# Queries and keys of a differential attention produced channel-major, rotated through a small DMA round trip

## The chip, the cores and the metric

The kernel runs on one core of a Trainium2 chip. The metric is device time in microseconds of one execution; three runs of the kernel before gave 909.8 to 910.3 us, median 910.19 us. A separate execution was profiled.

## The reference

Two layers over a sequence of 512 tokens and a width of 1024. A layer normalises the rows, multiplies them by a 1024 x 5120 matrix, and splits the result into ten blocks of 512 columns. Four mixers work on these: a state-space scan (S5), a differential attention with partial rotary positions, a gated linear recurrence (RG-LRU), and an attention into 256 memory tokens. Their gated results, 2048 wide, go through an output matrix and are added to the residual. The part that the change touches:

```python
for layer in range(DEPTH):                                   # DEPTH = 2
    h = rms_norm(x, norm_g[layer])
    proj = h @ w_in[layer]
    a_u, a_g, qd, kd, vd, b_g, c_x, c_g, m_q, m_g = jnp.split(proj, 10, axis=-1)
    ...
    q = rope_partial(qd.reshape(B, L, 4, 2, 64), cos, sin)   # turns dims 0..15 of each 64
    k = rope_partial(kd.reshape(B, L, 4, 2, 64), cos, sin)
    o_b = diff_attention(q, k, v, lam)       # softmax(q1 k1) - lam * softmax(q2 k2), causal
    y_b = rms_norm(o_b, da_subln_g[layer]) * (1 - lam_init)
```

## The kernel before

All large products are made with values split in two float32r parts: `w_split` casts a weight piece (128 x 1024) to `whi` on ACT (L168) and takes the remainder `wlo` on DVE (L174), and each product is three matmuls of 512 columns (high x high, high x low, low x high). A piece holds 24 matmuls, for memory values 12. There are 68 pieces a layer; raw pieces come by SP's queue into two buffers, `whi` and `wlo` have three buffers each, and DVE's and ACT's work for a piece is written two pieces ahead of its use.

A block of 512 projected columns is 96 matmuls. `tm_block` (L535) gives it token-major: a tile has 128 tokens in its partitions, four accumulators in PSUM are filled at once and evacuated at the block's end. `cm_block` (L515) gives it channel-major: a tile has 128 channels in its partitions and all 512 tokens along them; it goes in two units of two accumulators. `ORDER` lists the blocks of each layer by hand: `q v k kv cx au ...` in the first, `q k cx v kv au mq bg mg ...` in the second.

Between the matmuls, other work is written out by `Streams`: after every 12 matmuls of a block a `tick` goes by and each live generator makes one step; a generator that yields a number sleeps for so many ticks. A block of 512 columns is 8 ticks. Attention is such a stream, with an item (128 queries of one head, both softmaxes) every second tick, 16 items a layer and two further steps; S5, RG-LRU, the memory attention and the parameters are others. The compiler's scheduler then sets the order of each engine's instructions by this program order and by what it takes to be ready.

Before, q and k were made token-major. `qk_evac` copies an accumulator to `qz` (ACT, L575), multiplies dims 0 to 15 by cosines and sines (DVE, four small operations a token tile), and two ticks later `flush_qk` turns the tile to channel-major by four 128 x 128 transposes on TensorE (L595). From the transposed PSUM tile q is copied once (L598); k is copied and subtracted into two tiles `kT` whose halves hold its high and low parts (L603, DVE). `attention` starts when q, k and v are all there, which is after k in the first layer and after v in the second.

Tiles of 512 columns a partition that live long (`b8`) share 14 buffers, tiles of 4 KB (`b4`) four, tiles of 2 KB (`b2`) ten; in PSUM there are four accumulators (`acc`), two banks for transposes and small products (`tp` and `ms`), and one double bank for scores (`sc`).

At the start, SP's queue brings the first tile of x, constants, the second tile of x, the first weight piece, the third tile, the second piece and the fourth tile. `norm_h` and `transpose_split` normalise and transpose each tile.

Of the kernel before, what the change touches and what calls it, by code (L numbers as in the profile page):

```python
# [9 lines left out]
F32 = mybir.dt.float32  # L10
# [6 lines left out]
P = 128  # L17
D = 1024
# [8 lines left out]
ROPE_THETA = 500000.0  # L27


ORDER = ["q v k kv cx au cg bg mq ag mg gl oAM0 oAM1 oBC0 oBC1".split(),  # L30
         "q k cx v kv au mq bg mg ag cg gl oAM0 oAM1 oBC0 oBC1".split()]

C_ID, C_DM, C_IF, C_KEEP, C_CM, C_END = 0, 128, 144, 152, 152, 280

# [13 lines left out]


MEM_AHEAD = 2  # L50
BD_AHEAD = 3
S5P_AT = 2
D_MEM = (3, 2, 1)
D_S5 = (1, 1, 2, 2, 1, 2)
D_AT = 2


class Streams:
# [31 lines left out]
def tile_kernel(ctx: ExitStack, tc: tile.TileContext, A, out):  # L90
# [20 lines left out]
    def b8(shape, name, dtype=F32):  # L111
        return big.tile(shape, dtype, tag="b8", name=nm(name))
# [4 lines left out]
    def b2(shape, name, dtype=F32):  # L117
        return sm2.tile(shape, dtype, tag="b2", name=nm(name))
# [10 lines left out]
    def tp(shape=(P, 4, 128)):  # L129
        return ps.tile(list(shape), F32, tag="tp", bufs=2, name=nm("tp"))  # L130
# [13 lines left out]
    def w_dma(upto):  # L144

        while loaded[0] < min(upto, len(pieces)):
            w_load(loaded[0])
            loaded[0] += 1
# [12 lines left out]
    def w_split(i, pool_):  # L161

        while split[pool_] < min(i + 1, len(pieces)):
            j = split[pool_]
            split[pool_] += 1
            if pool_ == "hi":
                hi = wpool.tile([P, 1024], F32R, tag="whi", bufs=NHI, name=nm("whi"))
                S.copy(hi, wbuf[j])  # L168
                wbuf[j] = (wbuf[j], hi)
            else:  # L170
                w_split(j, "hi")
                raw, hi = wbuf[j]
                lo = wpool.tile([P, 1024], F32R, tag="wlo", bufs=NLO, name=nm("wlo"))
                V.tensor_tensor(out=lo, in0=raw, in1=hi, op=ALU.subtract)  # L174
                wbuf[j] = (hi, lo)
                w_dma(j + NRAW + 1)
# [5 lines left out]


    xr = A["x"].rearrange("o (t p) d -> p (o t) d", p=P)
    xd = ctx.enter_context(tc.tile_pool(name="xd", bufs=1, space=bass.MemoryType.DRAM)).tile([L, D], F32, tag="xd", name="xd")
    xdr = xd.rearrange("(t p) d -> p t d", p=P)
    xt = {}

# [32 lines left out]
    for l in range(DEPTH):  # L221
        for n in ORDER[l]:
            if n == "kv":
                for u in range(2):
                    add(l, "mk", u, cm_pieces(A["w_mem_kv"][l], 256 * u))
                add(l, "mv", 0, tm_pieces(A["w_mem_kv"][l], 512))
            elif n == "gl":
                w = A["s5_w_glu"][l].rearrange("(k p) (s c) -> p k s c", p=P, s=2)
                for u in range(2):
                    add(l, "gl", u, [w[:, 2 * i:2 * i + 2, :, 256 * u:256 * u + 256] for i in range(2)])  # L230
            elif n[0] == "o":
                ps_ = []
                for g in n[1:3]:
                    r0 = 512 * "ABCM".index(g)
                    ps_ += tm_pieces(w_out[l, r0:r0 + 512], 512 * int(n[3]))
                add(l, "o", n[1:], ps_)
            elif n in ("q", "k", "v", "au"):
                add(l, n, 0, tm_pieces(w_in[l], COL[n]))
            else:
                for u in range(2):  # L240
                    add(l, n, u, cm_pieces(w_in[l], COL[n] + 256 * u))
# [8 lines left out]
    S.dma_start(out=grow, in_=A["norm_g"][0:1, :])  # L250
    ident = cst[:, C_ID:C_ID + 128]
    nc.sync.dma_start(out=cst[:, C_ID:C_KEEP], in_=A["consts"][:, C_ID:C_KEEP])
    for t in range(1, NT):
        nc.sync.dma_start(out=xs(t), in_=xr[:, t, :])
        w_dma(t)
# [39 lines left out]
    def norm_h(t):  # L295

        h = b4([P, D], "h")
        r = rstd_of(xs(t), D, h)
        scale_h(h, t, r)
        return h  # L300
# [24 lines left out]

    new_hT()
    hn = norm_h(0)
    for t in range(NT):
        h, hn = hn, (norm_h(t + 1) if t + 1 < NT else None)
        transpose_split(h, cur["hi"], cur["lo"], t * 128)  # L330
        if t < 2:
            w_split(t, "lo")
# [16 lines left out]
    def tt(o, a, b, op):  # L349
        V.tensor_tensor(out=o, in0=a, in1=b, op=op)  # L350
# [63 lines left out]
    def params():  # L414
# [71 lines left out]
        V.tensor_scalar(out=cneg, in0=cpos, scalar1=-4.0, scalar2=None, op0=ALU.mult)  # L486
        V.tensor_scalar(out=cpos, in0=cpos, scalar1=4.0, scalar2=None, op0=ALU.mult)

    nsum = const.tile([P, NT], F32, tag="nsum", name="nsum")

    mrs = const.tile([P, 2], F32, tag="mrs", name="mrs")
# [30 lines left out]
    def tm_block(lhs, evac, ids, tiles=NT, late=False):  # L522


        hi, lo = lhs
        a = [acc() for _ in range(tiles)]
        np_ = len(ids)
        wv = {}

        def mm(p, t):  # L530
            whi, wlo = wv[p]
            for kk in range(2):
                k = 2 * p + kk
                for i, (h, w) in enumerate(((hi, whi), (hi, wlo), (lo, whi))):
                    PE.matmul(a[t], h(k, t), w[:, kk, :], start=(p == 0 and kk == 0 and i == 0),  # L535
                              stop=(p == np_ - 1 and kk == 1 and i == 2))
            if p == np_ - 1:
                evac(t, a[t])

        def take(p):  # L540
            wv[p] = [w.rearrange("p (k c) -> p k c", k=2) for w in w_use(ids[p])]

        for p in range(np_ - 2 if late else np_):
            take(p)
            for t in range(tiles):
                mm(p, t)
                if t % 2 == 1:
                    yield
        if late:
            take(np_ - 2)  # L550
            take(np_ - 1)
            for t in range(tiles):
                mm(np_ - 2, t)
                mm(np_ - 1, t)
                yield

    def h_cm():
        hi, lo = cur["hi"], cur["lo"]
        return (lambda k: hi[k // 4][:, k % 4, :]), (lambda k: lo[k // 4][:, k % 4, :])

    def h_tm():
        hi, lo = cur["hi"], cur["lo"]
        return ((lambda k, t: hi[k // 4][:, k % 4, t * 128:(t + 1) * 128]),
                (lambda k, t: lo[k // 4][:, k % 4, t * 128:(t + 1) * 128]))
# [4 lines left out]
        return ((lambda k, t: hi[k // 4][:, k % 4, t, :]), (lambda k, t: lo[k // 4][:, k % 4, t, :]))  # L569


    def qk_evac(dst):
        def f(t, a):
            z = b2([P, 8, 64], "qz")
            S.copy(z, a.rearrange("p (m d) -> p m d", d=64))  # L575
            z12 = z[:, :, 0:16].rearrange("p m (s f) -> p m s f", f=8)
            ca = rcos[:, t, :].unsqueeze(1).unsqueeze(1).to_broadcast([P, 8, 2, 8])
            sa = rsin[:, t, :].unsqueeze(1).unsqueeze(1).to_broadcast([P, 8, 2, 8])
            rab = b2([P, 2, 8, 2, 8], "rab")
            ra, rb = rab[:, 0], rab[:, 1]  # L580
            tt(ra, z12, ca, ALU.mult)
            tt(rb, z12, sa, ALU.mult)
            tt(z12[:, :, 0, :], ra[:, :, 0, :], rb[:, :, 1, :], ALU.subtract)
            tt(z12[:, :, 1, :], ra[:, :, 1, :], rb[:, :, 0, :], ALU.add)
            pend.append((dst, t, z, st.now))
        return f

    pend = []
    def flush_qk():

        while pend and st.now - pend[0][3] >= 2:
            dst, t, z, _ = pend.pop(0)
            pt = tp()
            for j in range(4):
                PE.transpose(pt[:, j, :], z[:, 2 * j:2 * j + 2, :].rearrange("p m d -> p (m d)"), ident)  # L595
            ts = slice(t * 128, (t + 1) * 128)
            if len(dst) == 1:
                S.copy(dst[0][:, :, ts], pt)  # L598
            else:

                for m in range(2):
                    own, oth = slice(m * 64, m * 64 + 64), slice(64 - m * 64, 128 - m * 64)
                    S.copy(dst[m][own, :, ts], pt[own])  # L603
                    tt(dst[m][oth, :, ts], pt[own], dst[m][own, :, ts], ALU.subtract)

    st.hook = flush_qk

    def attention(l, R):
        while pend or "par" in st.live:
            yield  # L610
        qT, kT, v = R["qT"][0], R["kT"], R["v"]
        o = qT
        R["o"] = o
        oss = const.tile([P, 16], F32, tag="oss", name=nm("oss"))
# [495 lines left out]
    def run(gen):  # L1110
        for _ in gen:
            st.tick()
# [30 lines left out]
    def s5p_start(l):  # L1143
        s5_load(l, Rl[l])
        st.start("s5p", s5_params(l, Rl[l]))

    st.start("par", params())
    s5p_start(0)
    for pi, (l, n, u, ids) in enumerate(plan):
        R = Rl[l]  # L1150
# [5 lines left out]
        if any(p[0] == l and p[1] == "cx" for p in plan[pi:pi + BD_AHEAD]) and "bd" not in R:  # L1156
            lru_load(l, R)
        if n in ("q", "k"):
            R[n + "T"] = [b8([P, 4, L], "qT")] if n == "q" else [b8([P, 4, L], "kT", F32R) for _ in range(2)]
            run(tm_block(h_tm(), qk_evac(R[n + "T"]), ids))  # L1160
        elif n == "v":
            vt = R["v"] = b8([P, NT, 512], "v")

# [78 lines left out]
        elif n == "gl":  # L1242
# [4 lines left out]
            for hf, pid in enumerate(ids):  # L1247
                whi, wlo = (w.rearrange("p (k s c) -> p k s c", k=2, s=2) for w in w_use(pid))
                for j in range(2):
# [13 lines left out]
                        ag = R["ag"][:, 2 * u + j, :]  # L1263
                        V.scalar_tensor_tensor(out=ag, in0=th, scalar=0.25, in1=ag, op0=ALU.mult, op1=ALU.mult)
                    st.tick()
        if n in ("q", "k", "v") and all(a in R for a in ("qT", "kT", "v")):
            st.start("attn", attention(l, R))
        if n == "o":
            pair, half = u[:2], int(u[2])
# [99 lines left out]
```

## Time and profile before

| | |
|---|---|
| median of three runs | 910.19 us |
| profiled execution | 911.01 us, of which the span from first to last instruction is 909.2 us |
| TensorE (PE) | busy 887.7 us, 98% |
| VectorE (DVE) | busy 667.3 us, 73% |
| ScalarE (ACT) | busy 510.7 us, 56% |
| GpSimd (POOL) | busy 42.2 us, 5% |
| DMA | 90.05 MB, 99 GB/s on average |
| granted clock of TensorE | 0.997 |

A busy PE is not a PE at its peak: matmuls are pipelined and each is shown with a duration longer than the distance to the next, so the distances between starts tell what one costs. Sums below are made against the profiled execution; the median of the runs is 0.8 us lower.

### The profile page before, as it was taken

What the parts mean: (1) busy time and instruction counts of PE and PEld (TensorE: products, weight loads), DVE (VectorE), ACT (ScalarE), POOL (GpSimd) and SP (SyncE); (2) the same over time, 40 slices, a digit from 0 to 9 for tenths busy, and PEclk for the clock granted to TensorE, in tenths of its full rate; (3) what the DMA queues carried; (4) which work ended last, traced back from release to release, by engine and by line L of the source; (5) the groups of instructions that cost most, each with busy time, mean ns of one, the idle gap of its engine ahead of it and who ended that gap; (6) DMA issues with size and microseconds to landing.
All of it is one profiled execution on the core that took longest, in us unless ns stands there. A gap on an engine that the chain in (4) does not pass through costs nothing.

```text
span 909.2 us, 12391 instructions
## 1 busy us (share of the span) xinstructions
PE 887.7 (98%) x4478; PEld 746.5 (82%) x4478; DVE 667.3 (73%) x1345; ACT 510.7 (56%) x1032; POOL 42.2 (5%) x86
## 2 busy tenths in 40 slices
PE   7999999999999999999999999999999999999996
PEld 5788878987878888888888888898888888788885
DVE  5984988778999956883384676875999996666343
ACT  5673786985344265921454468766656354863133
POOL 1001000001101100000100000000101110000000
PEclk9999999999999999999999999999999999999998
DMA  5743432022212236433343321432112222152322
GB/s 179 180 139 105 140 95 88 29 68 58 89 55 66 74 115 194 132 107 108 107 157 101 92 88 58 136 116 70 50 48 74 74 74 93 47 186 96 109 73 93
DMA packets 80929, 90.05 MB, mean 99 GB/s; under 512 B 23778, under 2 KB 58211, under 8 KB 80868
## 3 DMA queue, kind: packets, MB, share of 16 engines
q1 hardware_dynamic: 77842, 85.72, 30.1%
q10 hardware_dynamic: 722, 2.36, 0.8%
q0 software_dynamic: 2304, 1.18, 0.5%
q8 instruction: 35, 0.57, 0.3%
q14 instruction: 26, 0.21, 0.1%
HBM read 84.40 MB, written 4.19 MB: 97 GB/s over the span
## 4 chain that ended last, share of the span: by engine, by line
PE 73%; DVE 20%; ACT 5%; issue 2%; DMA 1%; SPq 0%; DVEq 0%; ACTq 0%
PE acc L535 38%; PE acc L515 16%; PE acc L1255 5%; DVE wlo L174 3%; DVE u L350 2%; DVE xr L1040 2%; DVE wt L350 2%; DVE xr L350 1%; PE ms L679 1%; PE tp L315 1%; PE sc L807 1%; PE sc L645 1%; PE tp L832 1%; PE sc L646 1%; DVE li L757 1%
## 5 line engine op out<-in xcount | busy, mean ns | idle before, releaser
L174 DVE TENSOR_TENSOR wlo<-raw,whi 128x1024 fp32r<-128x1024 f32 x136 | 166.0, 1221 | 120.8 <-ACT whi L168 117.0
L168 ACT CAST whi<-raw 128x1024 fp32r<-128x1024 f32 x136 | 143.2, 1053 | 190.4 <-PE acc L535 119.2
L515 PE MATMUL acc<-hThi,whi 128*128 128x512 f32 x384 | 153.3, 399 | 0.0
L515 PE MATMUL acc<-hThi,wlo 128*128 128x512 f32 x384 | 150.8, 393 | 0.0
L515 PE MATMUL acc<-hTlo,whi 128*128 128x512 f32 x384 | 150.6, 392 | 0.0
L535 PE MATMUL acc<-whi,hThi 128*128 128x512 f32 x256 | 104.1, 407 | 2.3 <-ACT whi L168 2.3
L535 PE MATMUL acc<-wlo,hThi 128*128 128x512 f32 x256 | 101.9, 398 | 0.0
L535 PE MATMUL acc<-whi,hTlo 128*128 128x512 f32 x256 | 101.1, 396 | 0.0
L535 PE MATMUL acc<-wlo,mxh 128*128 128x512 f32 x256 | 100.1, 391 | 0.0
L535 PE MATMUL acc<-whi,mxl 128*128 128x512 f32 x256 | 100.1, 391 | 0.0
L535 PE MATMUL acc<-whi,mxh 128*128 128x512 f32 x256 | 100.0, 391 | 0.0
L515 PEld LDWEIGHTS acc<-hThi,wlo 128*128 128x128 f32 x384 | 72.2, 188 | 14.8
L515 PEld LDWEIGHTS acc<-hTlo,whi 128*128 128x128 f32 x384 | 72.3, 188 | 13.3
L515 PEld LDWEIGHTS acc<-hThi,whi 128*128 128x128 f32 x384 | 72.2, 188 | 13.3
L535 PEld LDWEIGHTS acc<-whi,hThi 128*128 128x128 f32 x256 | 56.3, 220 | 10.3 <-ACT whi L168 2.7
L535 PEld LDWEIGHTS acc<-whi,hTlo 128*128 128x128 f32 x256 | 56.5, 221 | 7.8 <-DVE hTlo L318 0.2
L535 PEld LDWEIGHTS acc<-wlo,hThi 128*128 128x128 f32 x256 | 56.5, 221 | 7.2
L535 PEld LDWEIGHTS acc<-wlo,mxh 128*128 128x128 f32 x256 | 48.1, 188 | 9.8
L535 PEld LDWEIGHTS acc<-whi,mxl 128*128 128x128 f32 x256 | 48.1, 188 | 9.8
L535 PEld LDWEIGHTS acc<-whi,mxh 128*128 128x128 f32 x256 | 48.1, 188 | 9.6
L976 POOL DMA_DIRECT2D MT<-kq x64 | 32.1, 509 | 486.2 <-DVE kq L350 336.6
L655 ACT ACTIVATE e<-sc,nmx 128x128 f32<-128x128 f32 (+3 forms) x64 | 33.2, 528 | 10.3 <-DVE nmx L651 10.2
(313 smaller groups left out, 1643.1 us busy)
## 6 DMA issues: line engine op xcount, KB each, us to landing
raw<-in_w_in_dram SPq DMA_DIRECT2D x80, 512.0 KB, 3.6
raw<-in_w_out_dram SPq DMA_DIRECT2D x32, 512.0 KB, 3.4
raw<-in_w_mem_kv_dram SPq DMA_DIRECT2D x16, 512.0 KB, 3.3
x<-in_x_dram SPq DMA_DIRECT2D x8, 512.0 KB, 4.9
raw<-in_s_w_glu_dram SPq DMA_DIRECT2D x16, 256.0 KB, 3.2
mt<-in_mem_dram SPq DMA_DIRECT2D x4, 512.0 KB
xd<-x SPq DMA_DIRECT2D x4, 512.0 KB, 4.4
x<-xd SPq DMA_DIRECT2D x4, 512.0 KB, 5.5
```

Of the source, the lines that this page charges most:

```text
L168: S.copy(hi, wbuf[j])
L174: V.tensor_tensor(out=lo, in0=raw, in1=hi, op=ALU.subtract)
L315: lastins["pe"] = PE.transpose(pt[:, k, :], h[:, kk * 128:(kk + 1) * 128], ident)
L350: V.tensor_tensor(out=o, in0=a, in1=b, op=op)
L515: PE.matmul(a[j][:, :ncol], w[:, kk, c], h(k), start=(hf == 0 and i == 0), stop=(hf == 1 and i == 3 * nh - 1))
L535: PE.matmul(a[t], h(k, t), w[:, kk, :], start=(p == 0 and kk == 0 and i == 0), stop=(p == np_ - 1 and kk == 1 and i == 2))
L645: PE.matmul(s[:, m, :M], qh[:, m, h, :], kT[m][:, h, :M], start=True, stop=False)
L646: PE.matmul(s[:, m, :M], ql[:, m, h, :], kT[m][:, h, :M], start=False, stop=True)
L655: S.activation(e[:, m, :N], s[:, m, :N], AF.Exp, bias=nmx[:, m:m + 1], scale=0.125, accum_out=sm[:, m:m + 1])
L976: G.dma_start(out=MT[g * 64 + 64 - n:g * 64 + 64, g, t], in_=kq[g * 64:g * 64 + n])
L1040: V.tensor_tensor_scan(out=xr_[i][:, j, :], data0=dec, data1=xr_[i][:, j, :], initial=0.0, op0=ALU.mult, op1=ALU.add)
L1255: PE.matmul(a, w[:, k, s, j * 128:(j + 1) * 128], h[:, 2 * hf + k, :], start=(hf == 0 and i == 0), stop=(hf == 1 and i == 5))
```

## The change

q and k are made by `cm_block`, so that they come out channel-major and need no transposes: `z_evac` copies the accumulators into a long-lived tile `qz` or `kz` (partition = dim of one of a head's two halves, one 512-token row for each head). A new stream `rope` then turns 16 dims of each half: two DMAs on ACT's queue gather the 16 partitions x 4 heads of each half as 64 rows of 512 tokens (`rx`), DVE makes six operations (four of 32 x 512, two of 128 x 512) against tables of cosines and sines, and two DMAs on POOL's queue put the rows back. `D_ROPE` gives the ticks that the stream sleeps after each step. For k the split into `kT` follows, from SBUF. The tables are made once by the stream `rope_tables` (copies on POOL, eight transposes, copies on ACT), kept in DRAM, and loaded again in the second layer. `attention` starts after q and waits for both rotations.

The order becomes `v k q kv ...` and `v k cx q kv ...`. The load of RG-LRU's weights (`lru_load`) moves from three units ahead of `cx` to `cx` itself. At the start, the first weight piece is queued ahead of the second tile of x, and its cast to `whi` is written ahead of the second tile's normalisation. The attention's items, S5 and the rest are as before.

```diff
-ORDER = ["q v k kv cx au cg bg mq ag mg gl oAM0 oAM1 oBC0 oBC1".split(),
-         "q k cx v kv au mq bg mg ag cg gl oAM0 oAM1 oBC0 oBC1".split()]
+ORDER = ["v k q kv cx au cg bg mq ag mg gl oAM0 oAM1 oBC0 oBC1".split(),
+         "v k cx q kv au mq bg mg ag cg gl oAM0 oAM1 oBC0 oBC1".split()]
-BD_AHEAD = 3
+BD_AHEAD = 1
+D_ROPE = {"k": ((2, 3), (2, 3)), "q": ((4, 6), (3, 5))}
...
+    w_dma(1)
     for t in range(1, NT):
         nc.sync.dma_start(out=xs(t), in_=xr[:, t, :])
         w_dma(t)
...
     hn = norm_h(0)
+    w_split(0, "hi")
     for t in range(NT):
...
+    def rope_tables():
+        for w, src in enumerate((rcos, rsin)):
+            rep_ = b2([P, NT, P], "rep")
+            for i in range(NT):
+                G.tensor_copy(rep_[:, i].rearrange("p (a f c) -> p a f c", a=4, c=4),
+                              src[:, i].unsqueeze(1).unsqueeze(3).to_broadcast([P, 4, 8, 4]))
+            yield 2
+            pr = tp()
+            for i in range(NT):
+                PE.transpose(pr[:, i, :], rep_[:, i], ident)
...
+            rtab.append(tab)
+            G.dma_start(out=rtd[w], in_=tab)
...
-    def qk_evac(dst):
...
-    def flush_qk():
...
+    def rope(l, R, n):
+        z = R[n + "z"]
+        while "rtab" in st.live:
+            yield
+        if l and n == "k":
+            rtab[:] = [b2([P, L], f"rt{i}") for i in range(2)]
+            for w in range(2):
+                S.dma_start(out=rtab[w], in_=rtd[w])
+        x1, x2 = b2([P, L], "rx"), b2([P, L], "ry")
+        rows = [(x1[m * 64:m * 64 + 64], z[m * 64:m * 64 + 16]) for m in range(2)]
+        for x_, z_ in rows:
+            S.dma_start(out=x_, in_=z_)
+        yield D_ROPE[n][l][0]
+        co, si = rtab
+        for g in range(4):
+            to, fr = slice(g * 32, g * 32 + 32), slice((g ^ 1) * 32, (g ^ 1) * 32 + 32)
+            tt(x2[to], x1[fr], si[fr], ALU.mult)
+        tt(x1, x1, co, ALU.mult)
+        tt(x1, x1, x2, ALU.add)
+        for x_, z_ in rows:
+            G.dma_start(out=z_, in_=x_)
+        yield D_ROPE[n][l][1]
+        if n == "k":
+            kT = R["kT"] = [b8([P, 4, L], "kT", F32R) for _ in range(2)]
+            for h in range(0, 4, 2):
+                hs = slice(h, h + 2)
+                for m in range(2):
+                    own, oth = slice(m * 64, m * 64 + 64), slice(64 - m * 64, 128 - m * 64)
+                    S.copy(kT[m][own, hs], z[own, hs])
+                    tt(kT[m][oth, hs], z[own, hs], kT[m][own, hs], ALU.subtract)
+                yield
     def attention(l, R):
-        while pend or "par" in st.live:
+        while any(n in st.live for n in ("par", "ropeq", "ropek")):
             yield
...
+            def z_evac(j, a, u=u, zt=zt):
+                S.copy(zt[:, 2 * u + j, :], a)
+            run(cm_block(h_cm(), 8, z_evac, ids))
+            if u == 1:
+                st.start("rope" + n, rope(l, R, n))
...
-        if n in ("q", "k", "v") and all(a in R for a in ("qT", "kT", "v")):
+        if n == "q" and u == 1:
             st.start("attn", attention(l, R))
```

## Rows read from the trace of the kernel before

**Rows 1.** Page, part 1: busy time, share, instructions.
```profile
PE 887.7 (98%) x4478; PEld 746.5 (82%) x4478; DVE 667.3 (73%) x1345; ACT 510.7 (56%) x1032; POOL 42.2 (5%) x86
```

**Rows 2.** PE's waits over the span: who waited for whom, us, times, longest.
```profile
PE tp L669 <- DVE e L661: 3.0, 3, 1.7
```

**Rows 3.** Groups: shapes, count, busy us, mean ns, idle before and its releasers.
```profile
L595 PE MATMUL tp<-cst,qz 128*128 128x128 f32 x64 | 8.9, 274 | 2.1 <-DVE tA L350 1.3 <-DVE rden L350 0.4 <-DVE kT L350 0.4
```

**Rows 4.** Chain that ended last, second layer: start, us, what.
```profile
486.21 0.87 PE tp L595 x8
487.08 2.74 PE acc L535 x12
```

**Rows 5.** Groups of DVE work on q and k, columns as in rows 3.
```profile
L350 DVE TENSOR_TENSOR rab<-qz,cs 128x128 f32<-128x128 f32 x16 | 4.6, 287 | 3.8 <-ACT qz L575 3.8
L350 DVE TENSOR_TENSOR qz<-rab 128x64 f32<-128x64 f32 x32 | 5.9, 218 | 0.4
L350 DVE TENSOR_TENSOR kT<-tp,kT 64x512 fp32r<-64x512 f32 x16 | 10.7, 687 | 1.1 <-ACT kT L603 0.8
```

**Rows 6.** Stretches: us, then busy us and count of PE, PEld, DVE, ACT, POOL.
```profile
60.00:88.00 28.00, 28.00 (x135) 23.29 (x135) 13.98 (x44) 13.29 (x22) 1.87 (x4) 1.00 0.30 92
195.00:220.00 25.00, 23.34 (x137) 19.86 (x136) 22.14 (x36) 18.19 (x37) 4.03 (x8) 1.00 0.22 67
220.00:310.00 90.00, 88.27 (x475) 74.98 (x474) 88.96 (x173) 33.98 (x68) 12.01 (x24) 1.00 0.22 68
650.00:760.00 110.00, 109.43 (x616) 93.75 (x615) 108.27 (x210) 52.41 (x112) 15.01 (x30) 1.00 0.21 65
```

**Rows 7.** Attention's DVE work by shape, columns as in rows 3.
```profile
L350 DVE TENSOR_TENSOR sc<-sc,cmt 128x256 f32<-128x256 f32 x32 | 13.7, 427 | 10.4 <-PE sc L646 9.6 <-ACT jk L682 0.9
L649 DVE TENSOR_REDUCE mx<-sc 128x2 f32<-128x1024 f32 x8 | 9.7, 1217 | 0.1
L661 DVE SCALAR_TENSOR_TENSOR e<-e,cc 128x512 f32<-128x512 f32 x8 | 6.0, 746 | 0.1
L660 DVE TENSOR_SCALAR cc<-sm,nlam,rc 128x1 f32<-128x1 f32 x32 | 8.6, 269 | 0.7
```

**Rows 8.** PE in order of time around an item's products: start, duration.
```profile
661.72 0.40 PE L645 MATMUL sc<-kT,qh 128*128 128x512 f32 x1
...
662.64 0.39 PE L515 MATMUL acc<-hThi,wlo 128*128 128x512 f32 x1
...
688.06 1.05 PE L679 MATMUL ms<-v,pT 128*128 128x128 f32 x8
688.87 0.47 PE L515 MATMUL acc<-hThi,whi 128*128 128x512 f32 x1
...
691.72 0.39 PE L515 MATMUL acc<-hThi,whi 128*128 128x512 f32 x1
```

**Rows 9.** PE from 650 to 760 us: all its waits.
```profile
PE tp L669 <- DVE e L661: 0.4, 1, 0.4
```

**Rows 10.** Groups from 650 to 760 us, columns as in rows 3; first of three.
```profile
L515 PE MATMUL acc<-hThi,whi 128*128 128x512 f32 x110 | 44.0, 400 | 0.0
```

**Rows 11.** Start of the kernel, ACT and PE: start, duration, idle before.
```profile
8.19 1.06 ACT L288 ACTIVATE h<-x 128x1024 f32<-128x1024 f32 x1 [2.65 <-DMA x<-in_x_dram]
...
10.04 1.04 ACT L168 CAST whi<-raw 128x1024 fp32r<-128x1024 f32 x1
...
11.14 0.79 PE L535 MATMUL acc<-whi,hThi 128*128 128x512 f32 x1 [2.29 <-ACT whi L168]
```

**Rows 12.** Tiles kT and bg: operation, count, ns, first and last start.
```profile
L645 PE MATMUL sc<-kT,qh x64: 277/340/504, 91.8 to 667.5; 128*128 128x256 f32 x32, 128*128 128x384 f32 x16, 128*128 128x512 f32 x16
...
L717 DVE SCALAR_TENSOR_TENSOR bg<-th,acc x8: 657/680/689, 234.3 to 694.4; 128x512 f32<-128x512 f32 x8
```

**Rows 13.** Issues of DMAs: count, KB each, us to landing.
```profile
bd<-in_lru_w_a_dram POOLq DMA_DIRECT2D x4, 64.0 KB, 2.5
...
B<-in_s_b_re_dram SPq DMA_DIRECT2D x4, 128.0 KB, 5.2
```

More of the change, by code (lines that the diff above doesn't have):

```diff
@@ L184, in tile_kernel @@
     xr = A["x"].rearrange("o (t p) d -> p (o t) d", p=P)
-    xd = ctx.enter_context(tc.tile_pool(name="xd", bufs=1, space=bass.MemoryType.DRAM)).tile([L, D], F32, tag="xd", name="xd")
+    dpool = ctx.enter_context(tc.tile_pool(name="xd", bufs=1, space=bass.MemoryType.DRAM))
+    xd = dpool.tile([L, D], F32, tag="xd", name="xd")
     xdr = xd.rearrange("(t p) d -> p t d", p=P)
@@ L236, in tile_kernel @@
                 add(l, "o", n[1:], ps_)
-            elif n in ("q", "k", "v", "au"):
+            elif n in ("v", "au"):
                 add(l, n, 0, tm_pieces(w_in[l], COL[n]))
@@ L487, in params @@
         V.tensor_scalar(out=cpos, in0=cpos, scalar1=4.0, scalar2=None, op0=ALU.mult)
+    rtab = []
+    rtd = [dpool.tile([P, L], F32, tag=f"rtd{i}", name=f"rtd{i}") for i in range(2)]
+    def rope_tables():
[8 more added lines that the diff above has]
+                PE.transpose(pr[:, i, :], rep_[:, i], ident)
+            pf = pr.rearrange("p i c -> p (i c)")
+            tab = b2([P, L], f"rt{w}")
+            if w == 0:
+                S.copy(tab, pf)
+            else:
+                for g in range(4):
+                    r = slice(g * 32, g * 32 + 32)
+                    S.activation(tab[r], pf[r], AF.Copy, scale=-1.0 if g % 2 else 1.0)
+            rtab.append(tab)
+            G.dma_start(out=rtd[w], in_=tab)
     nsum = const.tile([P, NT], F32, tag="nsum", name="nsum")
@@ L569, in h_au @@
         return ((lambda k, t: hi[k // 4][:, k % 4, t, :]), (lambda k, t: lo[k // 4][:, k % 4, t, :]))
-    def qk_evac(dst):
[L573 to L586, printed above, removed]
@@ L588, in tile_kernel @@
-    pend = []
-    def flush_qk():
[L591 to L599, printed above, removed]
+    def rope(l, R, n):
[12 more added lines that the diff above has]
+        co, si = rtab
+        for g in range(4):
+            to, fr = slice(g * 32, g * 32 + 32), slice((g ^ 1) * 32, (g ^ 1) * 32 + 32)
[9 more added lines that the diff above has]
+                hs = slice(h, h + 2)
@@ L601, in flush_qk @@
                 for m in range(2):
                     own, oth = slice(m * 64, m * 64 + 64), slice(64 - m * 64, 128 - m * 64)
-                    S.copy(dst[m][own, :, ts], pt[own])
-                    tt(dst[m][oth, :, ts], pt[own], dst[m][own, :, ts], ALU.subtract)
-    st.hook = flush_qk
+                    S.copy(kT[m][own, hs], z[own, hs])
+                    tt(kT[m][oth, hs], z[own, hs], kT[m][own, hs], ALU.subtract)
+                yield
     def attention(l, R):
-        while pend or "par" in st.live:
+        while any(n in st.live for n in ("par", "ropeq", "ropek")):
@@ L610, in attention @@
             yield
-        qT, kT, v = R["qT"][0], R["kT"], R["v"]
+        qT, kT, v = R["qz"], R["kT"], R["v"]
         o = qT
@@ L1147, in tile_kernel @@
     st.start("par", params())
+    st.start("rtab", rope_tables())
     s5p_start(0)
@@ L1158, in tile_kernel @@
         if n in ("q", "k"):
-            R[n + "T"] = [b8([P, 4, L], "qT")] if n == "q" else [b8([P, 4, L], "kT", F32R) for _ in range(2)]
-            run(tm_block(h_tm(), qk_evac(R[n + "T"]), ids))
+            if u == 0:
+                R[n + "z"] = b8([P, 4, L], n + "z")
+            zt = R[n + "z"]
+            def z_evac(j, a, u=u, zt=zt):
[3 more added lines that the diff above has]
+                st.start("rope" + n, rope(l, R, n))
         elif n == "v":
```

## The prediction

> **What bounds the kernel now.** I read the page's busy line first: PE is busy for 887.7 of 909.2 us, DVE for 73%, ACT for 56% [rows 1]. That could still be a PE that waits a little everywhere, so I asked for PE's waits: the longest entry of the whole span is 3.0 us, three waits for the attention's `e` [rows 2]. The chain of waits in the q and k blocks is matmuls and transposes end to end: twelve matmuls in 2.74 us, 0.228 us each, then eight transposes in 0.87 us, 0.109 us each [rows 4]. The reader should see that there PE never waits, so work taken from PE is time. Then the stretches: from 220 to 310 us and from 650 to 760 us DVE has no free time either (88.96 of 90, 108.27 of 110), while from 60 to 88 us it is half idle [rows 6]. The two full stretches are where S5 runs, and where the attention of each layer ends. So the kernel has one bound, PE, and in two stretches a second one at almost the same height. A change pays what it takes from PE, less what it pushes into DVE's full stretches.
>
> **The change part by part.**
>
> *Transposes.* 64 go (four for each of four token tiles, for q and k, in two layers [rows 3]) and eight come for the tables: 64 x 0.109 - 8 x 0.109 = 6.1 us less on PE. The matmuls of a block stay 96, at the same distance. The count is safe, the price is worth a second look, because the group shows 274 ns for one transpose [rows 3] where the chain shows 109 ns [rows 4]; the first is a duration that overlaps the next instruction, the second is what PE's queue pays. The Trainium skill, TensorE: Matmul & The Clock Gate, Part 4: PE-mode transpose, gives about 275 ns for a transpose inside a kernel; the duration here agrees with it. Taken as a price, that would make it 56 x 0.275 = 15.4 us, an estimate from that page. I go by the distance.
>
> *Waits of these transposes.* PE stood 2.1 us ahead of them, nearly all in the first layer, for DVE, which was behind with the parameters (`tA`, `rden`) [rows 3]. All of it goes; the table's transposes need sines from the same busy stretch and may take back nothing or all 2.1 us. I take 0.5: -1.6 us.
>
> *The start.* ACT waits for the second tile of x until 8.19, squares it, then casts half of the first tile's `hThi`, then at 10.04 the first weights, and PE starts at 11.14 after 2.29 us of idling [rows 11]. With the weights queued ahead, they land where the tile did; cast from 8.2 to 9.2, `hThi` in the half microsecond behind it, first matmul near 9.9: 1.2 us gained. If ACT squares the late tile before it casts `hThi`, the start stays, or slips by the later landing, up to about 1.0 us (one square). I take -0.5.
>
> *DVE and ACT for the rotation.* Off: 16 pairs of 0.29 us and 32 of 0.218, together 15.2 us [rows 5]. On: four rotations of six 512-element operations at the 0.687 of the nearest row, 16.5 us [rows 5]. k's subtractions are half as many and twice as long. ACT loses q's second copies and gains ten DMA issues and the table's copies. All of it lies in stretches like 60 to 88 us, where DVE has 14.0 us free and ACT 14.7 of 28 [rows 6], so I take 0. Without that cover the difference of 1.3 us would count.
>
> *The round trips.* Sixteen DMAs of 128 KB, and four of 256 KB for the tables. The nearest landings are 2.5 us for 64 KB from POOL and 5.2 us for 128 KB in small pieces [rows 13]. A stream sleeps two to six ticks after each leg, at 2.74 us a tick [rows 4] at least 5.5 us: above both ends. If a leg is late, DVE stands at the first product, and behind it on its queue stand the `wlo` pieces, written two pieces (four ticks, 11 us) ahead of their use: a wait of some microseconds is hidden. ACT's issues wait only for its own copies and for a 2 KB buffer. On POOL's queue `lru_load` now stands ahead of k's return in the second layer, but `kT` is read 17 ticks later. I take 0; the bounds are 0 and one tick, 2.7 us, a stand that the weight buffers would not cover. The memory's normalisation, moved to q's second unit, has four ticks for three steps: 0, by the same bound.
>
> *The attention starts later.* This is the part that the diff doesn't show. Before, it starts one tick after the third block: tick 25 in the first layer (q, v, k of eight ticks each), 33 in the second (q, k, cx, v). After, q is third or fourth, and its rotation sleeps 4 + 6 or 3 + 5 ticks: ticks 35 and 41. Ten and eight ticks at one item in two: five and four items move behind, out of emptier stretches into the full ones. The last items cost DVE 0.43 + 1.22 + 0.75 and three small operations of at most 0.27 (I take 0.6 together): 3.0 us each [rows 7]. They cost PE 0.92 us of scores, four transposes of 0.109 and 0.81 for the values: 2.2 us [rows 8]; that PE work moves too and gives DVE time. First layer: 5 x 3.0 = 15.0 for DVE, less 5 x 2.2 = 11.0, less the 2.9 and 1.0 us that DVE has free from 195 to 310 [rows 6]: 0.1, rounded up to 1 since the free time is in pieces. Second layer: 4 x 3.0 and the split of one query block (four operations of 0.69), 14.7, less 8.8, less 1.7 free [rows 6]: 4.2. There PE waited 0.4 us in all 110 [rows 9], so work is done ahead by an amount that no row shows; I take 3. Together +4; the ends are 0 (all covered) and 12 (the first rival).
>
> Sum: -6.1 - 1.6 - 0.5 + 4 = -4.2 us, against the profiled execution's 911.0: 906.8. The median of the runs is 0.8 lower: 906.0.
>
> **The rivals.** All use the gains, 8.2 us.
>
> *A buffer comes free too late (slower).* I count the 14 long-lived tiles in the middle of the second layer: four of h, v, two `kT`, q (which becomes the output), two of the memory's keys and values, the recurrence's result, `U`, and two of the memory's queries: all 14. `bg` needs the next one, and `kT` gives it when the last item's scores are read. That is at 667.5 us now [rows 12]; `bg`'s two units fill the four accumulators, and the next block starts its matmuls at 691.7 [rows 8], with `bg`'s last evacuation at 694.4 [rows 12]. There are 24 us of room. Eight ticks are 96 matmuls; in 650 to 760 us PE went through three times 110 of these [rows 10], a piece of 24 in 8.0 us, so eight ticks are 32 us. That is 8 us over; and since the last two items still pass DVE's queue behind S5, about a chain of 4 us more: 12. Time: 911.0 - 8.2 + 12 = 914.8, as a median 914.0. For it speaks the count; against it, that an idle PE lets the last two items run early, and that the waiting time is DVE's to catch up. It decides if the last scores move by more than 24 us.
>
> *DVE's bound takes it all (no change).* If DVE's free pieces can't be used and nothing was done ahead, the shifted items cost 15.0 - 11.0 and 14.7 - 8.8: 9.9 us, 912.7, as a median 911.9. For it: 88.96 of 90 [rows 6]. Against: PE hardly waited for DVE there [rows 9].
>
> *The shift costs nothing.* 911.0 - 8.2 = 902.8, as a median 902.0. For it: rows 9 again, and that S5's results are needed only after the gates' blocks. Against: both engines full at once.
>
> *A transpose costs its duration.* Then the first term is 56 x 0.274, 15.3 us [rows 3], and the time 911.0 - 15.3 - 1.6 - 0.5 + 4 = 897.6, as a median 896.8. The chain, with the next matmul 0.87 us after eight transposes [rows 4], speaks against it. This is what the page's 275 ns would give.
>
> **How the numbers follow.** A measurement of this kernel can tell about 0.2% from no change, 1.8 us: below 908.4 is faster, above 912.0 slower. Forecast (903.5 to 908.4, the loss of 4 give or take 2.5): 0.42. No cost of the shift: 0.12. Transposes at their duration: 0.02. These are faster: 0.56. DVE takes it all, with the times between 908.4 and 912: 0.19, same. The late buffer: 0.25, slower. The range goes from 900.0 (902.0 less the 1.2 us start and the rest of the 2.1 us waits) to 915.0 (the late buffer's 914.0 and a microsecond of the trips), which leaves out some 0.04 below and 0.12 above. Cases of both signs hold much; the likeliest one's own range is 903.5 to 908.4.
>
> **What would show it.** PE's instructions down by 56; no wait at transposes of `qz`; the table's transposes near 25 to 40 us, with a wait under 2 us; the first matmul of weights near 10 us; the round trips landing in 2.5 to 5.2 us with no DVE wait on `rx` above a microsecond; the attention's first scores about ten ticks later in the first layer and eight in the second; DVE without a gap in both S5 stretches, and PE's waits there grown by about 4 us, on S5's transposes and on `wlo`. The prediction is wrong if PE stands at the first matmul after `bg` in the second layer for 5 us or more (the late buffer), or waits for the rotation, or for ACT's casts behind a DMA issue that waits.

## The result: 2.5% slower, and the profile after

The median is 933.54 us (931.91 to 935.05) against 910.25 us for the kernel before, run beside it: a ratio of 1.0254, with an interval of 1.0242 to 1.0266. The prediction was 906.0 us, faster. The profiled execution took 931.91 us with a span of 930.1, so 20.9 us more than the span before.

The page's busy line (part 1) is to be read against [rows 1]. Below it stands the clock row of part 2: the granted clock in 40 equal slices of the span, in tenths.

```profile
PE 890.1 (96%) x4422; PEld 744.4 (80%) x4422; DVE 669.6 (72%) x1297; ACT 510.3 (55%) x1021; POOL 50.4 (5%) x104
...
PEclk9999999999999999999999998999987999999999
```

PE has 56 instructions fewer, as the count of transposes said. It is busy for 2.4 us more all the same, and idles for 40 us instead of 21.5; in slices 25, 30 and 31 (of 23.3 us each) its granted clock dips. Where it idles stands in PE's waits over the whole span (waiter, who it waited for, us, times, longest), to be read against [rows 2], whose longest entry was 3.0:

```profile
PE acc L566 <- DVE kv L355: 6.9, 1, 6.9
PE tp L699 <- DVE e L691: 4.5, 2, 3.1
PE sc L675 <- ACT e L685: 4.3, 2, 3.9
PE sc L675 <- DVE u L355: 2.6, 1, 2.6
```

Two places, then. The first entry is one wait of 6.9 us at the first matmul of the second layer's memory values. The others lie nearly all close together near the end of the second layer's attention, as the stretches show (columns as in [rows 6]). A third, smaller place in the first layer comes up further below.

```profile
550.00:580.00 30.00, 22.03 (x143) 19.90 (x142) 25.66 (x34) 18.31 (x26) 1.03 (x2) 0.92 0.38 106
650.00:684.00 34.00, 33.60 (x187) 28.24 (x187) 33.71 (x69) 17.82 (x42) 3.96 (x8) 1.00 0.16 48
684.00:710.00 26.00, 14.10 (x58) 10.26 (x58) 22.07 (x46) 8.18 (x22) 0.05 (x1) 0.67 0.14 43
710.00:760.00 50.00, 49.89 (x294) 42.85 (x293) 38.42 (x76) 30.49 (x69) 4.01 (x8) 1.00 0.18 55
```

From 684 to 710 us PE runs 58 instructions at a mean clock of 0.67. The kernel before put 145 into the same stretch:

```profile
684.00:710.00 26.00, 25.85 (x145) 21.72 (x144) 25.75 (x51) 17.84 (x40) 4.01 (x8) 1.00 0.28 84
```

PE, DVE, PE's weight loads and ACT in order of time at the end of that stretch (start, duration, engine, line, idle before and its releaser) name the chain:

```profile
682.99 0.39 PE L546 MATMUL acc<-hThi,wlo 128*128 128x512 f32 x1
...
706.80 0.63 PE L676 MATMUL sc<-kT,ql 128*128 128x512 f32 x1
...
707.46 1.88 DVE L747 SCALAR_TENSOR_TENSOR bg<-th,acc 128x512 f32<-128x512 f32 x3 [0.43 <-PE sc L676]
...
708.20 0.19 PEld L546 LDWEIGHTS acc<-hThi,whi 128*128 128x128 f32 x1 [0.65 <-DVE bg L747]
...
708.32 0.59 ACT L1038 COPY yg<-tp 128x512 f32<-128x512 f32 x1 [0.99 <-PE sc L676]
```

`bg`'s last matmul starts at 682.99. Its four accumulators are full, and `bg` gets a buffer only when the last scores have read the first `kT` (706.80 + 0.63 = 707.43). Three hundredths later DVE evacuates `bg`, and PE goes on. The second `kT` is handed on in the same way: S5's output `yg` is first written at 708.32, when the scores that start at 707.65 have read it. This is the late buffer of the rivals; the time in which PE has little to start because of it is called the stand below. Its rows, beside [rows 12], where the last scores start at 667.5 and `bg`'s last evacuation at 694.4:

```profile
L675 PE MATMUL sc<-kT,qh x64: 278/334/794, 108.3 to 707.2; 128*128 128x256 f32 x32, 128*128 128x384 f32 x16, 128*128 128x512 f32 x16
...
L747 DVE SCALAR_TENSOR_TENSOR bg<-th,acc x8: 670/682/689, 229.6 to 709.3; 128x512 f32<-128x512 f32 x8
```

The first wait has its chain on DVE (DVE in order of time, then PE):

```profile
567.00 2.77 DVE L355 TENSOR_TENSOR ry<-rx,rt 32x512 f32<-32x512 f32 x4
...
575.00 1.22 DVE L787 TENSOR_TENSOR_SCAN li<-lr,xc 128x512 f32<-128x512 f32 x1
576.26 1.42 DVE L355 TENSOR_TENSOR kv<-acc,kv 128x256 fp32r<-128x256 f32 x4
```

```profile
569.63 0.28 PE L546 MATMUL acc<-mhi,wlo 128*128 128x256 f32 x1
576.83 0.77 PE L566 MATMUL acc<-whi,mhi 128*128 128x512 f32 x1 [6.92 <-DVE kv L355]
577.39 0.63 PE L566 MATMUL acc<-wlo,mhi 128*128 128x512 f32 x1
577.82 0.63 PE L566 MATMUL acc<-whi,mlo 128*128 128x512 f32 x1
```

The memory's keys were multiplied by 569.9, but DVE could write `kv` only at 576.26, right behind the last scan of RG-LRU, among whose scans the six operations of q's rotation now lie. Before, that last scan ran at 570.1 and the first `kv` followed at 571.4, so PE, coming later, did not wait.

The 20.9 us can be laid out by the first matmuls of the blocks, which I found in the timeline by counting the matmuls of each block. All in the second layer, in us:

| stretch | before | after | change |
|---|---|---|---|
| start of the kernel to the layer's first matmul | 462.1 | 459.8 | -2.3 |
| four blocks of projections | 101.0 | 97.1 | -3.9 |
| memory's keys and values | 28.2 | 34.2 | +6.0 |
| `au` and `mq` | 63.4 | 58.2 | -5.2 |
| `bg` | 37.0 | 58.9 | +21.9 |
| behind `bg` to the end | 217.5 | 221.9 | +4.4 |

(The second row is q, k, cx, v before, and v, k, cx, q after; the attention starts behind them in both.) The gain of the second row is there; that of the first is within the spread of such profiles (459.2 to 462.6 us, as told further below). Both are lost at the `kv` wait, seem to come a second time in `au` and `mq`, which the late attention has left, and are lost several times over in `bg`.

### The profile page after: what moved, and what is told of

Same layout as the page of the kernel before. It is cut to its first block, busy times and chain, and to the rows that moved or that the text cites. A ratio compares the mean times of both kernels' runs of the same rounds, so it can differ in the third digit from the quotient of the medians.

```text
span 930.1 us, 12250 instructions
## 1 busy us (share of the span) xinstructions
PE 890.1 (96%) x4422; PEld 744.4 (80%) x4422; DVE 669.6 (72%) x1297; ACT 510.3 (55%) x1021; POOL 50.4 (5%) x104
## 4 chain that ended last, share of the span: by engine, by line
PE 67%; DVE 22%; ACT 7%; issue 2%; DMA 2%; ACTq 0%; DVEq 0%; SPq 0%
PE acc L566 27%; PE acc L546 23%; PE acc L1293 5%; DVE wlo L175 4%; DVE u L355 2%; DVE xr L1070 2%; DVE wt L355 1%; ACT whi L169 1%; PE ms L709 1%; DVE xr L355 1%; PE tp L319 1%; DVE xp L355 1%; DMA raw<-in_w_mem_kv_dram 1%; PE sc L675 1%; PE tp L862 1%
## 5 line engine op out<-in xcount | busy, mean ns | idle before, releaser
L546 PE MATMUL acc<-hThi,whi 128*128 128x512 f32 x512 | 203.8, 398 | 0.7 <-ACT v L1203 0.7
L546 PE MATMUL acc<-hTlo,whi 128*128 128x512 f32 x512 | 201.5, 394 | 0.0
L546 PE MATMUL acc<-hThi,wlo 128*128 128x512 f32 x512 | 201.3, 394 | 0.0
L546 PEld LDWEIGHTS acc<-hThi,whi 128*128 128x128 f32 x512 | 96.3, 188 | 19.9 <-ACT v L1203 1.1
L546 PEld LDWEIGHTS acc<-hTlo,whi 128*128 128x128 f32 x512 | 96.4, 188 | 18.2
L566 PE MATMUL acc<-whi,hThi 128*128 128x512 f32 x128 | 53.0, 415 | 0.0
L685 ACT ACTIVATE e<-sc,nmx 128x128 f32<-128x128 f32 (+3 forms) x64 | 33.3, 527 | 34.5 <-DVE nmx L681 34.3
L566 PE MATMUL acc<-whi,hTlo 128*128 128x512 f32 x128 | 51.6, 405 | 0.0
L566 PE MATMUL acc<-wlo,hThi 128*128 128x512 f32 x128 | 51.5, 403 | 0.0
L566 PEld LDWEIGHTS acc<-whi,hTlo 128*128 128x128 f32 x128 | 32.2, 251 | 3.1 <-DVE hTlo L322 0.7
L566 PEld LDWEIGHTS acc<-wlo,hThi 128*128 128x128 f32 x128 | 32.3, 252 | 2.4
```

Source lines behind the costliest of these rows:

```text
L546: PE.matmul(a[j][:, :ncol], w[:, kk, c], h(k), start=(hf == 0 and i == 0), stop=(hf == 1 and i == 3 * nh - 1))
L685: S.activation(e[:, m, :N], s[:, m, :N], AF.Exp, bias=nmx[:, m:m + 1], scale=0.125, accum_out=sm[:, m:m + 1])
```

## The experiments

The theory: the two waits are waits for buffers, with two owners. `kT` gives its buffer up when the attention ends, which is late because the attention starts late; RG-LRU gives one up when its scans end, at DVE's pace. The main rival: DVE is the bound of these stretches, the waits are only where it shows, and taking one away moves the loss. Ratios are against the kernel before, with intervals.

**The lateness alone**, put into the kernel before:

```diff
 def attention(l, R):
...
+        if l:
+            yield 8
```

> The kernel before with one line more: the second layer's attention sleeps eight ticks before its first item; q, k and their rotation stay token-major. If the late release of kT's buffer is the cause, the block bg of the second layer grows from 37 us by about 20 us (it was 58.9 us in the changed kernel), PE stands at the first matmul behind bg, and the time is 928 to 932 us. If it is DVE's work that is pushed into the full stretch, the loss is 3 to 6 us and spread over bg, mg and ag: 913 to 916 us. If it is the rotation's round trips, nothing changes: 910 us.

Measured: 926.66 us, 1.0173 (1.0158 to 1.0189), a little under the 928 to 932 expected of the late buffer; the block `bg` takes 59.5 us. `bg` asks for its buffer at the same place, and the waits from 640 to 705 us are those of the changed kernel, though no rotation and no new DMA is in this one. The waits, and the stretch of the stand:

```profile
PE tp L671 <- DVE e L663: 4.5, 2, 3.1
PE sc L647 <- ACT e L657: 3.9, 1, 3.9
PE sc L647 <- DVE u L350: 2.6, 1, 2.6
...
684.00:705.00 21.00, 11.11 (x32) 7.72 (x33) 16.50 (x35) 7.54 (x21) 0.00 (x0) 0.55 0.05 17
```

DVE is idle for 4.5 of these 21 us, so it is not full either: the last items pass PE, DVE and ACT one after another, with S5's operations between theirs on DVE, and PE has little else to do. Lateness alone makes 15.9 of the 23.3 us lost. Whether it does so by the buffer or by DVE is for the next but one run to tell.

**The same in the first layer**, by 10 ticks:

```diff
 def attention(l, R):
...
+        if not l:
+            yield 10
```

> The kernel before with one edit: in the first layer the attention sleeps 10 ticks at its start (tick 35 instead of 25, as in the changed kernel). My prediction priced this at about 1 us with ends 0 and 4 (15.0 of DVE less 11.0 of PE); the changed kernel's first layer as a whole came out near what it was. Expected 909 to 914 us. If the first layer has a late buffer too, which the other edits of the changed kernel cover, 915 us or more.

Measured: 911.31 us, 1.0012 (1.0002 to 1.0022), some 1 us. In that layer `cg` stands ahead of `bg`, and no late buffer shows.

**The buffer of `bg`**, in the changed kernel, by the order of the second layer's later blocks:

```diff
-         "v k cx q kv au mq bg mg ag cg gl ...".split()]
+         "v k cx q kv au cg bg mq ag mg gl ...".split()]
```

> The changed kernel with only the order of the second layer's later blocks altered (cg bg mq ag mg instead of mq bg mg ag cg), so that the gate cg frees the recurrence's buffer before bg asks for one; the attention still starts at tick 41. Late buffer: bg no longer needs the buffer that kT holds, the stand of about 22 us in the second layer's bg goes, and the time is 912 to 918 us. DVE's bound (the late items simply do not fit): the stand only moves to another wait on DVE, and the time stays above 925 us.

Measured: 920.59 us, 1.0103 (1.0088 to 1.0119): 13.0 us better than the changed kernel, a little short of what I expected of the theory (912 to 918), and below the 925 of the rival. The last evacuation of `bg` now comes well ahead of the last scores, and PE waits 0.3 us from 645 to 690 us, with a clock of 1.00:

```profile
L747 DVE SCALAR_TENSOR_TENSOR bg<-th,acc x8: 675/680/690, 232.4 to 697.5; 128x512 f32<-128x512 f32 x8
...
L676 PEld LDWEIGHTS sc<-kT,ql x64: 186/188/330, 111.3 to 712.1; 128*128 128x128 f32 x64
...
645.00:690.00 45.00, 44.70 (x246) 37.55 (x244) 42.81 (x87) 24.96 (x62) 8.04 (x16) 1.00 0.18 51
```

The attention ends later than ever (712.1), and PE no longer stands for its end: the block `bg` takes 34.5 us instead of 58.9, with the same work on DVE. So it was the buffer. Of the 24 us that `bg` loses, some 10 come back in other blocks: the first output block alone takes 32.3 us in this order and 21.8 in the other. (The first layer, which has this order too, shows 32.5 there.) The `kv` wait of 6.9 us is unchanged in this run, as it should be.

**The buffer of `kv`**, by starting the recurrence a block earlier:

```diff
-         "v k cx q kv au mq bg ...".split()]
+         "v cx k q kv au mq bg ...".split()]
```

> The changed kernel with the second layer's order v cx k q kv: the recurrence (RG-LRU) starts and ends a block of 22 us earlier, the attention starts at the same tick 41. If the 6.9 us wait at the first matmul of the memory values is a buffer that the recurrence holds until its scans end, that wait goes and the time falls by 4 to 7 us, to 926 to 929 us, with bg still near 58 us. If that wait is the rotation of q taking DVE's time, it stays (q's rotation lies in the same place), and the time stays within 2 us of 933.

Measured: 927.58 us, 1.0182 (1.0167 to 1.0197), 6.0 us better. From 550 to 600 us no wait of PE is longer than 1.0 us. q's rotation still lies in the block of the memory's keys (its first products at 560.9 to 564.5 us, at 567.0 to 569.8 in the changed kernel), so it is the scans' place that counts.

**Both orders together:** `"v cx k q kv au cg bg mq ag mg gl ..."`.

> The changed kernel with both orders in the second layer: v cx k q kv, and cg bg mq ag mg behind au. The attention still starts at tick 41. If the two waits are buffers of two different owners and nothing else, their gains add (13 and 6 us): 912 to 916 us. If the attention's lateness costs by DVE as well, it stays above the kernel before by more than the gains of the start and the transposes allow, at 917 us or more.

Measured: 914.32 us, 1.0037 (1.0024 to 1.005), 19.2 us better than the changed kernel. The two alone gave 13.0 + 6.0 = 19.0, and the time lies in the 912 to 916 expected. The gains add: two waits, two owners.

**The recurrence a block later instead**, with the attention as early as before:

```diff
-         "v k cx q kv au mq bg ...".split()]
+         "v k q cx kv au mq bg ...".split()]
```

> The changed kernel with the second layer's order v k q cx kv: the attention starts at tick 33, the tick of the kernel before, and cx still stands ahead of the memory's keys. Lateness alone as the cause: bg near 37 to 40 us, the gains of the transposes and the start remain, and the time is 903 to 910 us. If DVE's bound in the second layer takes the gains (as the 914.9 us of the order v k q kv cx suggests), 911 to 917 us. If the recurrence, now a block later, holds the memory values' buffer, a wait of some microseconds shows there.

Measured: 932.45 us, 1.0229 (1.0213 to 1.0244). I had expected 903 to 910 if only the attention's lateness counted; what came is the last case of the expectation, far larger than the "some microseconds" there. From 553 to 602 us, while the memory's keys wait, PE does little over half a stretch's work. The timelines of ACT and DVE show `kv` behind the last scan again; ACT writes the high part of `kv`, DVE the low part, which is a tile of its own:

```profile
553.00:602.00 49.00, 27.46 (x164) 23.50 (x163) 39.36 (x75) 40.28 (x86) 0.00 (x0) 0.75 0.23 64
...
581.66 0.43 ACT L823 CAST kv<-acc 128x256 fp32r<-128x256 f32 x1
...
600.02 1.21 DVE L787 TENSOR_TENSOR_SCAN li<-lr,xc 128x512 f32<-128x512 f32 x1
...
601.27 1.42 DVE L355 TENSOR_TENSOR kv<-acc,kv 128x256 fp32r<-128x256 f32 x4
```

The last high part is written at 581.66, so one of the two tiles had its buffer. The low parts wait until the scan has ended (600.02 + 1.21 = 601.23), although DVE is idle for 9.6 of the 49 us, 3.7 of them behind 582, and the four operations take 1.42: a wait for a buffer, and not for DVE. The stand in `bg` is gone in this kernel, since the attention starts early (37.0 us). The second buffer costs more here than the first did: the block of the keys takes 48.0 us, 14.5 before.

**q and the memory ahead of the recurrence:** `"v k q kv cx au mq bg mg ag cg gl ..."`.

> The changed kernel with the second layer in the order v k q kv cx: attention starts at tick 33 there, as in the kernel before, and RG-LRU after the memory's blocks; everything of the rotation stays. Late buffer: bg is back at 37 to 40 us, and the wait of the memory's values for RG-LRU's buffers (6 us) goes as well: 908 to 914 us. DVE's bound or the rotation's own cost: above 922 us.

Measured: 914.9 us, 1.0048 (1.003 to 1.0066). Neither wait is left: the longest of PE from 530 to 785 us is 2.9, for ACT's cast of q, and `bg` takes 39.4 us. With them 18.6 us of the loss are gone.

**Shorter sleeps of q's rotation**, so that the attention starts earlier in both layers:

```diff
-D_ROPE = {"k": ((2, 3), (2, 3)), "q": ((4, 6), (3, 5))}
+D_ROPE = {"k": ((2, 3), (2, 3)), "q": ((1, 2), (1, 2))}
```

> The changed kernel with q's sleeps cut from 4 and 6, and 3 and 5, ticks to 1 and 2 in both layers: attention starts seven ticks earlier in the first layer and five in the second, with the same DMAs. Late buffer: bg of the second layer shrinks from 58.9 us by five ticks of some 3.5 us, to about 41 to 44 us, and the time is 915 to 920 us. If the round trips need the sleeps, DVE stands on rows that have not landed and the time stays above 928 us.

Measured: 922.6 us, 1.013 (1.0116 to 1.0144). That lies between the two cases expected. Seven ticks in the first layer and five in the second repay nearly half of the loss. The second layer's `bg` falls further than expected, to 30.7 us. In exchange the first layer ends at 468.4 us instead of 459.8: it has a stretch with a clock of 0.89 (255 to 285 us), and 3.7 us of a wait for `wlo` came up.

**Both orders and the shorter sleeps in the second layer only:** `"v cx k q kv au cg bg ..."` and `"q": ((4, 6), (1, 2))`.

> As the run before this one, and in the second layer q's rotation sleeps 1 + 2 ticks instead of 3 + 5, so that the attention starts about tick 36. Lateness: another 2 to 6 us off, 907 to 913 us, the best version of the change. If the rotation's trips need the longer sleeps here, DVE or PE waits for rx or qz and the gain is lost: 914 us or more.

Measured: 912.37 us, 1.0018 (1.001 to 1.0027), the best version of the change: 1.7 us behind the kernel before, and not ahead of it.

**Is DVE the bound of what is left?** The order `v k q kv cx`, without the addition of the causal mask in the second layer:

```diff
-            tt(s[:, :, i * 128:N], s[:, :, i * 128:N], bc(cmt, 1, [P, 2, P]), ALU.add)
+            if not l:
+                tt(s[:, :, i * 128:N], s[:, :, i * 128:N], bc(cmt, 1, [P, 2, P]), ALU.add)
```

> The order v k q kv cx of the second layer (914.9 us, no late buffer), and the second layer's attention leaves out the addition of the causal mask: 16 operations of 0.43 us less on DVE, 6.8 us, and nothing less on PE. If DVE is the bound of the stretch from au to gl, the time falls by 4 us or more, to 911 us or less. If PE is the bound there, it stays within 1.5 us of 914.9.

Measured: 913.21 us, 1.003 (1.0018 to 1.0041), against 1.0048 (1.003 to 1.0066) with the mask. The medians are 1.7 us apart and the intervals overlap, so 6.8 us less on DVE bring nothing that is clear of the noise, and by the ends of the intervals 4.4 us at most. (Eleven of the 16 additions, 4.7 us, lay behind the start of `au`; the rest lay ahead of it.) The 911 us or less expected of a DVE that bounds the whole stretch isn't reached. A part that DVE bounds is not excluded.

**The start alone**, in the kernel before:

```diff
+    w_dma(1)
     for t in range(1, NT):
...
+    w_split(0, "hi")
```

> The kernel before with the start of the changed one alone: the first weights queued ahead of the second tile of x, and their cast written ahead of its square. In the changed kernel the first matmul of weights stands at 8.7 us instead of 11.1. If PE's order from there on is the same, the gain stays: 908 us. If the later tiles of x arrive later and PE waits for them, it is given back within the first block: 910 us.

Measured: 909.47 us, 0.9984 (0.9975 to 0.9993). The first weight matmul starts at 9.62 in the profile, instead of 11.14. These two lines are the only version whose interval lies below the kernel before, by 0.16%.

**RG-LRU's weights as early as before**, one of the smaller edits undone:

```diff
-BD_AHEAD = 1
+BD_AHEAD = 3
```

> The changed kernel with one of its smaller edits undone: RG-LRU's weights are loaded three units ahead of cx again. I priced this edit at nothing: 932 to 935 us. If the later load holds up the recurrence in the second layer, and with it the memory values' buffer, 927 to 930 us.

Measured: 939.23 us, 1.0317 (1.0303 to 1.033), a miss both ways: this edit, which I had at nothing, was worth some 5.7 us to the changed kernel. The `kv` wait is 6.9 us here too. In the profile the loss is in the first layer, where the attention's first scores come at 115.1 instead of 108.3. DVE comes to q's rotation later there, and its way back is issued at 105.23 instead of 101.04. What puts the rotation later isn't settled.

## Why the prediction was wrong

*The step that failed* is "Second layer: ... Together +4", with its rival. The prediction counted the 14 tiles, named `bg` and `kT`, and drew the line at "the last scores move by more than 24 us". They moved by 39.7 us (667.5 to 707.2), and the rival was what happened. It had 0.25. Three things were wrong with the two figures:

- Its size. I turned eight ticks into 32 us by the pace of 650 to 760 us, where PE never stood. Once `bg`'s accumulators are full, PE's only work is the last items' own chain, so the shift no longer runs at PE's pace. I took 4 us for the last two items' chain. In fact the scores of the last three items start at 690.35, 695.62 and 706.22, with S5's operations between theirs on DVE. The rival priced the stand at 12 in all; the block `bg` grew by 21.9.
- What stood against it. "An idle PE lets the last two items run early": PE was idle, and the items did not run early, since DVE, busy 22.07 of 26 us with S5's operations and theirs, reached them no sooner. DVE sets how late the last item is; that PE must stand until then is the buffer's doing, as the run with the other order of the gates shows.
- The clock. In the stretch of the stand the granted clock is 0.67 on average, and matmuls of 512 columns, 0.23 us apart at 682.5, are 0.43 us apart in its last scores (706.80, 707.22, ...) and behind the `kv` wait (577.39, 577.82, ...). The prediction had no term for it.

*A second buffer that I didn't look for.* I listed what each tile is and asked only who is served last. RG-LRU's buffers go to the memory's keys and values, and the prediction's own gains bring PE there 6 us earlier, while q's rotation delays the scans. "All of it lies in stretches like 60 to 88 us ... so I take 0" failed here: the rotation's DVE time was covered in PE's sense, but it stood ahead of the last scan. (Its sum for the operations that go, 15.2 us, is near their busy time; by the counts and means given there it is 16.3. The measured rotation is 16.4.)

*A wait for q in the first layer.* The prediction took 0 for the round trips, 2.7 us at most, and named a wait for the rotation as a sign of being wrong. In the first layer PE stands for 2.2 and 1.0 us at the first scores, for ACT's and DVE's split of the rotated q (views of POOL, ACT and PE in order of time):

```profile
101.04 1.07 POOL L625 DMA_DIRECT2D qz<-rx  x2 [23.55 <-DVE kv L355]
...
106.08 1.04 ACT L169 CAST whi<-raw 128x1024 fp32r<-128x1024 f32 x1 [4.81 <-DMA raw<-in_w_mem_kv_dram]
107.03 0.61 ACT L659 CAST qh<-qz 64x512 fp32r<-64x512 f32 x1
...
108.34 0.38 PE L675 MATMUL sc<-kT,qh 128*128 128x256 f32 x1 [2.22 <-ACT qh L660]
```

The way back is issued from 101.04 on, and the slowest landing of such a trip is 5.6 us; ACT's cast of a weight piece, which waited for its own DMA, ends within the same microsecond. Which of the two holds q here is not shown. With the shorter sleeps q is back at 103.5 us, the cast ends at 106.0, and PE still stands for 2.0 us: there it is the cast, and not the trip. In the changed kernel the first layer's block of the memory's values takes 16.7 us, against 13.8 before and 11.4 with the late attention alone. Counted from its first weight matmul the first layer takes 451.1 us, and 450.9 before: the transposes saved in it bring nothing that is left at its end.

*Right:* The transposes cost their distance, as far as the second layer shows it. From the second layer's first matmul through its first three blocks, ahead of the recurrence's products (q, k, cx; then v, k, cx), the time went from 71.6 to 67.5 us, 4.1 less for 32 transposes, with whatever else differs between the blocks; at 0.109 us they are 3.5, at 0.274 they would be 8.8. The Trainium skill, TensorE: Matmul & The Clock Gate, Part 4: PE-mode transpose, has about 275 ns for one; as a price in a full queue this case bears out less than half of it. The first layer's lateness: +1 predicted, 1.1 us measured alone. The table's transposes ran from 31.8 us without a wait.

*Off in size:* The start. ACT did not square the late tile first: `whi` was cast at 6.73, and the first matmul came at 8.68, 2.5 us early and not 0.5. How much of this is the edit is less sure: in the other profiles the same start gives 8.68 to 10.06, and the old one 10.10 to 11.14. Alone it was 1.5 us in the profile and 1.25 by the medians. The trips landed in 3.1 to 5.6 us, a little above the bounds at the top, and DVE waited 2.8 us at the longest for `rx`, not below one (issues with their median landing; the group of the first products; the last line is of the tile `qz`):

```profile
rx<-kz ACTq DMA_DIRECT2D x4, 128.0 KB, 5.0
kz<-rx POOLq DMA_DIRECT2D x4, 128.0 KB, 3.4
rx<-qz ACTq DMA_DIRECT2D x4, 128.0 KB, 3.1
qz<-rx POOLq DMA_DIRECT2D x4, 128.0 KB, 4.5
...
L355 DVE TENSOR_TENSOR ry<-rx,rt 32x512 f32<-32x512 f32 x16 | 10.9, 683 | 6.2 <-DMA rx<-kz 3.5 <-DMA rx<-qz 2.5
...
DMA to landing us min/median/max: 3.1/3.6/5.6
```

*What stays open:* The best version of the change, without either stand, should by the gains of transposes and start be some 7 us ahead of the kernel before. It is 1.7 us behind. A part lies in the first layer, where it has the same wait for q (2.2 and 1.0 us, with a clock of 0.91 from 100 to 120 us). Profiles of kernels with the same first layer also put its end between 459.2 and 462.6 us, so part of the difference may be that. In its second layer, 448.2 us long against 447.2 before, the waits that are left are each at most 1.1 us. Taking 6.8 us from DVE brought little in another order, so DVE's bound alone doesn't explain it; the rest is not shown. Whether a fifteenth buffer would do what the orders did wasn't tried.

## What to carry to other kernels

Where a pool of buffers is full, the time at which each owner lets go is part of the critical path, even if nothing waits for it now: list for every long tile who gets its buffer next, and ask of any change what moves the last reader and what brings the next writer forward. Work taken from the bounding engine brings it to such a hand-over earlier, and the gain can end there. An order of blocks that lets a third tile go first can be worth more than the operations saved: here `cg` ahead of `bg`, and the recurrence first, took back 13.0 and 6.0 us, and all the transposes were priced at 6.1.

## What was not expected of the hardware

A stand of PE costs more than its length: behind the 6.92 us wait the next matmuls of 512 columns start 0.43 us apart for some 5 us, against 0.23 at 682.5, and the stretch's granted clock is 0.92 (550 to 580 us). Twelve matmuls at 0.2 us more each are some 2.4 us on top of the wait, an estimate from these distances. 0.43 is the pace at the lower of the clock's two levels, 1.2 GHz. The Trainium skill, TensorE: Matmul & The Clock Gate, Part 1 ("Wait — 56ns, not 53.3ns?"), gives 426.7 ns from start to start for 512 columns at that level, and the trace agrees.
